# A PEER expert layer: the second token block takes its second-table rows one by one, and all first-table tiles run before the second table

## The chip, the cores and the metric

The kernel runs on one core of a Trainium2 chip. The metric is the device time in microseconds, from the first to the last instruction; three runs gave 1636.88 to 1640.48 us, the median is 1637.82 us.

## What is computed

One decoder layer on 512 tokens of 1024 numbers, in float32: a token-mixing part (attention in a window beside causal pooling), then a retrieval part (PEER) over 128 x 128 = 16384 experts, then a norm. The change is in the retrieval part alone. It picks 16 experts for each of 8 heads and each token, 128 in all, and for each takes a dot product with the expert's row of a first table `u`, and adds the expert's row of a second table `v` with that weight:

```python
def chunk(xc):                                   # 128 tokens
    q = (xc @ w_query).reshape(c, PEER_HEADS, 2, D_HALF)
    sc = jnp.einsum('chpd,hpkd->chpk', q, sub_keys)
    sv, si = lax.top_k(sc, PEER_TOPK)            # 16 of 128 keys, in both halves
    ...                                          # 256 sums, the 16 best
    idx = jnp.take_along_axis(cidx, fi, axis=-1) # expert = 128 i + j
    g = jax.nn.softmax(fv, axis=-1)
    u = u_tab[idx]
    a = jax.nn.gelu(jnp.einsum('chkd,cd->chk', u, xc), approximate=False)
    vv = v_tab[idx]
    return jnp.einsum('chk,chkd->cd', (g * a), vv)
```

## The kernel before

The 512 tokens are four blocks of 128. Block 0 (`GB`) is done by fetching: `gather` fetches for each of its 128 slots one row of 4 KB per token from `u` with an indirect DMA that POOL issues (128 rows, 512 KB), takes the dot product on VectorE (L715), and later fetches the row of `v` and adds it, weighted, to `hg` (L719). Four buffers hold rows (`ROWS`).

Blocks 1 to 3 (`ND` = 3, 384 columns) are done densely. A **first-table tile** (`u_part`) multiplies 128 experts' rows of `u` with all 384 tokens on TensorE, and ScalarE applies Gelu (L604). A **second-table tile** (`v_mm`) multiplies 128 experts' weights, [expert, token], with 128 rows of `v`, and adds into three accumulators in PSUM. There are 128 tiles of either kind. Each product is three matmuls of a high and a low part (`mm3`), so a first-table tile has 8 x 3 = 24 matmuls of 384 columns and a second-table tile 3 x 2 x 3 = 18 of 512. The parts are made by ScalarE, which casts (L118), and VectorE, which subtracts (L110); `w` and `v` tiles have three or two buffers.

What an expert weighs for a token is spread into a dense table by one-hots: `select` finds a block's experts on VectorE, `onehot` builds for eight tokens at a time a one-hot of j (`ohj`) and one of i, weighted (`ohi`), and TensorE multiplies them (`pg`, L584); ScalarE copies the product (`gs`, L585) and SP sends it to DRAM (`spill`). `mix` reads it back (`gt`), multiplies it with the Gelu (L640) and casts (L642). Of every two builds one makes `ohj` on ScalarE (eight Abs of 128 columns, one Relu of 1024), the other on VectorE (`OHN`, `OHA`).

The order: a scheduler places the instructions of the routing stage on in-order queues; in the second-table stage TensorE, VectorE and ScalarE keep the order of the code (`manual_schedule`). `Background` gives out the steps of the selections, of the one-hots and of the fetches in credits for each first-table tile: 2.9 of routing (`R_A`) and 1.1 fetches (`G_A`). So 104 first-table tiles run before and while the routing runs, then comes the second table, and the last 24 first-table tiles stand inside it (`G_V`, `G_B` set the fetches there). Results of the first table that are made ahead lie in SBUF (14 tiles, `RES`) or go to DRAM and back (`ahead`).

## Time and profile before

| | |
|---|---|
| median of three runs | 1637.82 us |
| span of the profiled execution | 1638.0 us |
| TensorE busy | 1593.2 us, 97% |
| VectorE busy | 1260.9 us, 77% |
| ScalarE busy | 760.3 us, 46% |
| POOL busy | 323.0 us, 20% |
| moved by DMA | 403.43 MB, mean 246 GB/s |

A busy share is a mean over stages; for TensorE it is the time in which any matmul's record runs, and records overlap, so the pace is read from how many matmuls a stretch holds. The stages: mixing to about 350 us, scores to 475, block 0's selection to 530, the selections and one-hots of the dense blocks with first-table tiles to 986, the second table to 1620, the last norms.

### The profile page before, as it was taken

The numbers are of one execution on the slowest core, as the hardware profiler recorded it, in microseconds if no ns is written. First come the engines' busy times: TensorE is split into PE (matmuls) and PEld (weight loads), VectorE is DVE, ScalarE is ACT, GpSimd is POOL, SyncE is SP. The second block draws the span as 40 slices with busy tenths as digits, with TensorE's granted clock in tenths as the row PEclk, the third lists the DMA queues.
The fourth block names the chain that finished last, engine by engine and source line by source line (L and its number), as shares of the span: only waits on it lengthen the run. The fifth ranks groups of instructions, "written<-read, shape, count | busy, mean of one in ns | idle before, by whom it ended". The sixth has DMA issues, their size and how long they took to land.

```text
span 1638.0 us, 23397 instructions
## 1 busy us (share of the span) xinstructions
PE 1593.2 (97%) x8389; PEld 1411.9 (86%) x8389; DVE 1260.9 (77%) x2614; ACT 760.3 (46%) x1197; POOL 323.0 (20%) x262
## 2 busy tenths in 40 slices
PE   7999999999999899999999999999999999999997
PEld 6777788888899899999999998878888888899996
DVE  4676433546799899999999866877878878888885
ACT  4655533333333333894598863333333333433334
POOL 0000000000000334223322221221222222244440
PEclk9999999999999999999999999999999999999999
DMA  6111222531324888888988889999999999999983
GB/s 218 65 65 52 78 92 101 180 116 65 116 91 140 296 305 295 300 310 307 312 313 308 289 299 345 300 340 352 349 337 346 359 336 342 338 327 335 323 293 115
DMA packets 168117, 403.43 MB, mean 246 GB/s; under 512 B 14784, under 2 KB 87232, under 8 KB 164800
## 3 DMA queue, kind: packets, MB, share of 16 engines
q1 hardware_dynamic: 130384, 265.07, 46.1%
q0 software_dynamic: 36864, 134.23, 23.9%
q10 hardware_dynamic: 752, 2.62, 0.5%
q8 instruction: 66, 1.08, 0.3%
q14 instruction: 51, 0.42, 0.1%
HBM read 354.81 MB, written 46.53 MB: 245 GB/s over the span
## 4 chain that ended last, share of the span: by engine, by line
PE 86%; DMA 4%; DVE 4%; ACT 4%; issue 2%; SPq 0%; POOL 0%; DVEq 0%; ACTq 0%; POOLq 0%
PE mm L105 16%; PE mm L106 15%; PE mm L107 15%; PE acc L106 10%; PE acc L107 10%; PE acc L105 9%; PE pg L584 5%; DMA vr<-v_experts 2%; PE ho L105 1%; PE ho L107 1%; PE ho L106 1%; PE pss L453 1%; PE mm L368 1%; DVE wl L110 1%; ACT ohj L568 1%
## 5 line engine op out<-in xcount | busy, mean ns | idle before, releaser
L105 PE MATMUL mm<-xh,wh 128*128 128x384 f32 (+2 forms) x1424 | 503.3, 354 | 11.5 <-ACT ga L604 9.3
L107 PE MATMUL mm<-xh,wl 128*128 128x384 f32 (+2 forms) x1424 | 495.1, 348 | 1.9 <-DVE wl L110 1.9
L106 PE MATMUL mm<-xl,wh 128*128 128x384 f32 (+2 forms) x1424 | 494.8, 348 | 0.6 <-DVE xl L110 0.6
L110 DVE TENSOR_TENSOR wl<-wr,wh 128x1024 fp32r<-128x1024 f32 x187 | 228.0, 1220 | 135.7 <-ACT wh L118 123.0
L118 ACT CAST wh<-wr 128x1024 fp32r<-128x1024 f32 x187 | 195.6, 1047 | 284.9 <-PE mm L106 249.4
L709 POOL DMA_INDIRECT row<-u_experts,ei x128 | 150.0, 1172 | 885.5 <-ACT wh L118 528.2
L106 PE MATMUL acc<-vl,wh 128*128 128x512 f32 x768 | 299.9, 391 | 2.4 <-DVE vl L110 2.2
L107 PE MATMUL acc<-vh,wl 128*128 128x512 f32 x768 | 299.4, 390 | 0.0
L105 PE MATMUL acc<-vh,wh 128*128 128x512 f32 x768 | 298.8, 389 | 0.0
L105 PEld LDWEIGHTS mm<-xh,wh 128*128 128x128 f32 x1424 | 270.1, 190 | 31.0 <-ACT ga L604 10.7
L107 PEld LDWEIGHTS mm<-xh,wl 128*128 128x128 f32 x1424 | 269.8, 189 | 16.4 <-DVE wl L110 2.7
L106 PEld LDWEIGHTS mm<-xl,wh 128*128 128x128 f32 x1424 | 270.4, 190 | 13.8 <-DVE xl L110 1.1
L709 POOL DMA_INDIRECT row<-v_experts,ei x128 | 172.3, 1346 | 388.3 <-DVE hg L719 354.8
L642 ACT CAST wh<-wf 128x384 fp32r<-128x384 f32 x128 | 65.8, 514 | 322.5 <-PE acc L106 236.1
L110 DVE TENSOR_TENSOR vl<-vr,vh 128x1024 fp32r<-128x1024 f32 x128 | 156.7, 1224 | 52.8 <-ACT vh L118 49.7
L106 PEld LDWEIGHTS acc<-vl,wh 128*128 128x128 f32 x768 | 144.2, 188 | 33.9 <-DVE vl L110 4.6
L107 PEld LDWEIGHTS acc<-vh,wl 128*128 128x128 f32 x768 | 144.2, 188 | 29.8
L105 PEld LDWEIGHTS acc<-vh,wh 128*128 128x128 f32 x768 | 144.2, 188 | 29.5
L719 DVE SCALAR_TENSOR_TENSOR hg<-row,act,hg 128x1024 f32<-128x1024 f32 x128 | 163.6, 1278 | 2.9 <-DMA row<-v_experts,ei 2.5
L715 DVE SCALAR_TENSOR_TENSOR row<-row,natg 128x1024 f32<-128x1024 f32 x128 | 155.5, 1216 | 8.8 <-DMA row<-u_experts,ei 8.8
L118 ACT CAST vh<-vr 128x1024 fp32r<-128x1024 f32 x128 | 134.1, 1048 | 24.4 <-DMA vr<-v_experts 17.8
L110 DVE TENSOR_TENSOR wl<-wf,wh 128x384 fp32r<-128x384 f32 x128 | 74.0, 578 | 42.1 <-ACT wh L642 40.8
(179 smaller groups left out, 1611.6 us busy)
## 6 DMA issues: line engine op xcount, KB each, us to landing
wr<-u_blocks SPq DMA_DIRECT2D x128, 512.0 KB
vr<-v_experts SPq DMA_DIRECT2D x128, 512.0 KB
spill<-gs SPq DMA_DIRECT2D x24, 1024.0 KB
gt<-spill SPq DMA_DIRECT2D x64, 384.0 KB
ahead<-ga SPq DMA_DIRECT2D x90, 192.0 KB
gar<-ahead SPq DMA_DIRECT2D x90, 192.0 KB
wr<-w_in SPq DMA_DIRECT2D x30, 512.0 KB
wr<-w_query SPq DMA_DIRECT2D x16, 512.0 KB
```

Source lines behind the costliest of these rows:

```text
L105: mm(out, lhsT=l[0], rhs=r[0], start=first, stop=False)
L106: mm(out, lhsT=l[0], rhs=r[1], start=False, stop=False)
L107: mm(out, lhsT=l[1], rhs=r[0], start=False, stop=last)
L110: self.lowered = self.nc.vector.tensor_tensor(lo, src, hi.bitcast(F32), op=ALU.subtract).ins
L118: self.nc.scalar.copy(hi, raw)
L368: nc.tensor.matmul(po[half * 64:half * 64 + 64], lhsT=vn[:, b - 1 + k, kv * 64:kv * 64 + 64], rhs=pT[:, k, 2 * half:2 * half + 2, :], star ...
L453: nc.tensor.matmul(pss[n][b // 2][:, b % 2, i - n, :], lhsT=qT[:, b * P:(b + 1) * P], rhs=subk[:, i, :], start=True, stop=True)
L584: nc.tensor.matmul(pg[:, z, :], lhsT=ohj[:, z, :], rhs=ohi[:, z, :], start=True, stop=True)
L642: nc.scalar.copy(wh, wf)
L709: nc.gpsimd.indirect_dma_start(out=t, out_offset=None, in_=tab, in_offset=bass.IndirectOffsetOnAxis(ap=ei[:, s:s + 1], axis=0))
L715: nc.vector.scalar_tensor_tensor(u, u, 1.0, xn2, op0=ALU.mult, op1=ALU.mult, accum_out=act[:, s:s + 1])
L719: nc.vector.scalar_tensor_tensor(z, v, act[:, s:s + 1], z, op0=ALU.mult, op1=ALU.add)
```

## The change

Block 1 (`LB`) is taken out of the second table. Its first table stays dense: a tile still has 384 columns (`TU`), but the Gelu of block 1's 128 columns is written to a DRAM array of its own, `late`, [expert, token], four tiles at a time (`AJ`). Once all of it is there, `gather_late` fetches each of block 1's 128 x 128 activations singly: an indirect DMA for each slot takes one element per token, at the address 128 expert + token (`ea`). VectorE scales them and adds the fetched rows of `v` to `h1`. The dense second table, its one-hots and gates cover blocks 2 and 3 (`NV` = 2, 256 columns).

All 128 first-table tiles run before the second table. Block 0's fetches are given 2.3 credits a tile and are ended with the first table. 90 tiles' results stay in SBUF (4, 40 and 46), 38 go through DRAM. `ohj` is made by ScalarE in every build, now with the gate's weight in it (a second activation for each of the eight tokens), and `ohi` on VectorE by one comparison over 1024 columns in place of eight.

```diff
-ND = 3
+LB = 1
+VB = 2
+NV = 2
+TU = SEQ - P
+TD = NV * P
+AJ = 4
-R_A = 2.9
-G_A = 1.1
+R_A = 3.0
+G_A = 2.3
+LAG = 8
+R_F = 2.9
+KEEP = 4
+HELD = (40, 46)
-OHN, OHA = 2, 1
...
         def build(n):
-            if n % OHN < OHA:
-                for z in range(8):
-                    nc.scalar.activation(ohj[:, z, :], self.iota, AF.Abs, bias=tr[:, 1, u + z:u + z + 1])
-                nc.scalar.activation(ohj, ohj, AF.Relu, bias=1.0, scale=-1.0)
-            else:
-                v.tensor_tensor(ohj, iob, tr[:, 3, u:u + 8].unsqueeze(2).to_broadcast([P, 8, P]), op=ALU.is_equal)
+            for z in range(8):
+                nc.scalar.activation(ohj[:, z, :], self.iota, AF.Abs, bias=tr[:, 1, u + z:u + z + 1])
+            for z in range(8):
+                nc.scalar.activation(ohj[:, z, :], ohj[:, z, :], AF.Relu, bias=tr[:, 2, u + z:u + z + 1],
+                                     scale=tr[:, 3, u + z:u + z + 1])
-            for z in range(8):
-                v.tensor_scalar(ohi[:, z, :], self.iota, tr[:, 0, u + z:u + z + 1], tr[:, 2, u + z:u + z + 1],
-                                op0=ALU.is_equal, op1=ALU.mult)
+            v.tensor_tensor(ohi, iob, tr[:, 0, u:u + 8].unsqueeze(2).to_broadcast([P, 8, P]), op=ALU.is_equal)
...
+    def u_part(self, n, w, xn2):
+        ps = self.project(w, xn2, slice(LB * P, LB * P + TU))
+        if n % AJ == 0:
+            self.a1 = self.ga.tile([P, AJ, P], F32, name="a1", bufs=2)
+        nc.scalar.activation(self.a1[:, n % AJ, :], ps[:, :P], AF.Gelu)
+        if n % AJ == AJ - 1:
+            nc.sync.dma_start(out=self.late.rearrange("(n j t) o -> n j (t o)", j=P, t=P)[n - AJ + 1:n + 1]
+                              .rearrange("n j t -> j n t"), in_=self.a1)
...
+        nc.scalar.activation(ga, ps[:, P:], AF.Gelu)
...
+    def dense(self, acc, fetch):
+        rate = PH * TOPK / (NKEY - 3 - LAG)
         for n in range(NKEY):
             m = n + 1
+            if m < NKEY:
+                step = self.mix(m)
                 next(step)
                 next(step)
                 v_low = self.v_load(m)
+                if m >= LAG:
+                    fetch.spend(rate)
                 next(step, None)
                 v_low()
             self.v_mm(n, self.ws.pop(n), self.vs.pop(n), acc)
...
+    def gather_late(self, ei, ea, g, z):
+        act = self.dp.tile([P, PH * TOPK], F32, name="act1", bufs=1)
+        def elem(s):
+            nc.gpsimd.indirect_dma_start(out=act[:, s:s + 1], out_offset=None, in_=self.late,
+                                         in_offset=bass.IndirectOffsetOnAxis(ap=ea[:, s:s + 1], axis=0))
+        for k in range(TOPK):
+            elem(k)
+        yield 0
+        for h in range(PH):
+            hs = slice(h * TOPK, (h + 1) * TOPK)
+            nc.vector.tensor_tensor(act[:, hs], act[:, hs], g[:, hs], op=ALU.mult)
+            for s in range(h * TOPK, (h + 1) * TOPK):
+                if h + 1 < PH:
+                    elem(s + TOPK)
+                v = self.rows_of(self.a["v_experts"], ei, s)
+                nc.vector.scalar_tensor_tensor(z, v, act[:, s:s + 1], z, op0=ALU.mult, op1=ALU.add)
+                yield 1
...
-            bg = Background(choose(1), choose(2), spread(1), choose(3), spread(2), spread(3))
+            bg = Background(choose(2), choose(3), spread(2), choose(LB), spread(3))
...
+        rest = (2 * PH * TOPK - fetch.spent) / max(1, NKEY - ahead)
+        while ahead < NKEY:
+            with tc.issue_after(part()):
+                fetch.spend(rest)
+        fetch.spend(1e9)
```

The engines' queues show what the scheduler makes of it at three places. On ScalarE, in a one-hot stage, the kernel before has this (`wh` are casts of first-table weights, `ga` Gelus, `gs` copies of a product):

```order
L585 COPY gs_5915<-pg_5916 128x8x128
L568 ACTIVATE ohj_5963<-iota_155,tr3_5753 128x128 x8
L569 ACTIVATE ohj_5963<-ohj_5963 128x1024
L118 CAST wh_6145<-wr_6144 128x1024
L604 ACTIVATE ga_5960<-mm_5935 128x384
L585 COPY gs_5915<-pg_5982 128x8x128
L585 COPY gs_6004<-pg_6005 128x8x128
L568 ACTIVATE ohj_6052<-iota_155,tr3_5753 128x128 x8
L569 ACTIVATE ohj_6052<-ohj_6052 128x1024
L118 CAST wh_6234<-wr_6233 128x1024
L604 ACTIVATE ga_6049<-mm_6024 128x384
```

The changed kernel, in the second half of its first one-hot stage (`a1` is the Gelu of block 1):

```order
L603 ACTIVATE a1_6450<-mm_6425 128x128
L612 ACTIVATE ga_6452<-mm_6425 128x256
L570 ACTIVATE ohj_6455<-iota_155,tr3_5866 128x128 x8
L572 ACTIVATE ohj_6455<-ohj_6455,tr3_5866 128x128 x8
L585 COPY gs_6399<-pg_6474 128x8x128
L121 CAST wh_6845<-wr_6844 128x1024
L738 ACTIVATE act_4535<-act_4535 128x16
L603 ACTIVATE a1_6450<-mm_6499 128x128
L612 ACTIVATE ga_6525<-mm_6499 128x256
L570 ACTIVATE ohj_6528<-iota_155,tr3_5866 128x128 x8
L572 ACTIVATE ohj_6528<-ohj_6528,tr3_5866 128x128 x8
L585 COPY gs_6547<-pg_6548 128x8x128
```

Between two copies stand sixteen activations of 128 columns in place of none, or eight and one long one. In the first half of this stage eight builds follow each other with two casts among them and no Gelu.

On POOL, where the second table begins, the kernel before goes on with block 0's rows:

```order
L709 DMA row_9244<-v_experts,ei0_2733 128x1024
L709 DMA row_9281<-u_experts,ei0_2733 128x1024
L709 DMA row_9302<-v_experts,ei0_2733 128x1024
L709 DMA row_9336<-u_experts,ei0_2733 128x1024
L709 DMA row_9370<-v_experts,ei0_2733 128x1024
L709 DMA row_9404<-u_experts,ei0_2733 128x1024
```

The changed kernel has block 1's single elements there, 128 of them among the first 36 rows of `v`:

```order
L690 DMA row_10400<-v_experts,ei0_2733 128x1024
L690 DMA row_10445<-v_experts,ei1_2734 128x1024
L690 DMA row_10651<-v_experts,ei1_2734 128x1024
L690 DMA row_10681<-v_experts,ei1_2734 128x1024
L699 DMA act1_10426<-late,ea_2741 128x1 x20
L690 DMA row_10710<-v_experts,ei1_2734 128x1024
L699 DMA act1_10426<-late,ea_2741 128x1
L690 DMA row_10739<-v_experts,ei1_2734 128x1024
L699 DMA act1_10426<-late,ea_2741 128x1 x31
L690 DMA row_10768<-v_experts,ei1_2734 128x1024
```

A row whose turn comes after a group of single elements is issued after them.

On VectorE, at the same place, the kernel before has this (`wf` is a gate product, `vl` a split of the second table):

```order
L110 TENSOR_TENSOR wl_9249<-wr_9247,wh_9248 128x1024
L715 SCALAR_TENSOR_TENSOR row_9281,act_4502<-row_9281,natg_2379 128x1024
L640 TENSOR_TENSOR wf_9057<-gk0_2970,gt_9052 128x384
L640 TENSOR_TENSOR wf_9292<-gk1_3241,gt_9052 128x384
L719 SCALAR_TENSOR_TENSOR hg_76<-row_9302,act_4502,hg_76 128x1024
L110 TENSOR_TENSOR wl_9059<-wf_9057,wh_9058 128x384
L110 TENSOR_TENSOR wl_9294<-wf_9292,wh_9293 128x384
L110 TENSOR_TENSOR vl_9299<-vr_9297,vh_9298 128x1024
L640 TENSOR_TENSOR wf_9326<-gk2_3512,gt_9052 128x384
L715 SCALAR_TENSOR_TENSOR row_9336,act_4502<-row_9336,natg_2379 128x1024
```

In the changed kernel, where the second table's splits are named `wl<-wr`, it is this:

```order
L751 TENSOR_TENSOR ssf_10453<-ssf_10453 128x1
L753 RECIPROCAL rf_10455<-sdf_10454 128x1
L755 SCALAR_TENSOR_TENSOR fin_10452<-hg_76,rf_10455,gfin_10409 128x512 x2
L647 TENSOR_TENSOR wf_10423<-gk0_2978,gt_10418 128x256
L647 TENSOR_TENSOR wf_10469<-gk1_3250,gt_10418 128x256
L115 TENSOR_TENSOR wl_10425<-wf_10423,wh_10424 128x256
L115 TENSOR_TENSOR wl_10471<-wf_10469,wh_10470 128x256
L115 TENSOR_TENSOR wl_10476<-wr_10474,wh_10475 128x1024
L647 TENSOR_TENSOR wf_10494<-gk2_3522,gt_10418 128x256
L707 TENSOR_TENSOR act1_10426<-act1_10426,gw1_2738 128x16
L712 SCALAR_TENSOR_TENSOR h1_10411<-row_10445,act1_10426,h1_10411 128x1024
L115 TENSOR_TENSOR wl_10496<-wf_10494,wh_10495 128x256
```

The seventh row from the first `wf` on scales the first 16 single activations of block 1 and stands ahead of the splits for the third tile; the addition of a row, in each tile of the kernel before, is there in one tile of the first seven.

## Rows read from the trace of the kernel before

**Rows 1.** The page: engine, busy us (share of the span), x instructions.

```profile
PE 1593.2 (97%) x8389; PEld 1411.9 (86%) x8389; DVE 1260.9 (77%) x2614; ACT 760.3 (46%) x1197; POOL 323.0 (20%) x262
```

**Rows 2.** Busy time by stretch: us, engines (x instructions), granted clock, DMA share, GB/s.

```profile
core 0: us, PE busy (x) PEld busy (x) DVE busy (x) ACT busy (x) POOL busy (x), PEclk, DMA share, GB/s
...
530.00:661.00 131.00, 123.45 (x694) 121.74 (x693) 122.87 (x314) 47.45 (x65) 56.81 (x37) 0.97 0.88 298
...
798.00:986.00 188.00, 182.87 (x1233) 181.36 (x1232) 159.42 (x357) 155.53 (x238) 47.33 (x34) 1.00 0.85 302
993.00:1420.00 427.00, 423.63 (x1861) 350.08 (x1862) 345.84 (x457) 152.74 (x211) 93.81 (x97) 1.00 0.98 340
1420.00:1620.00 200.00, 200.00 (x1012) 182.09 (x1011) 161.04 (x190) 76.28 (x106) 80.78 (x60) 1.00 0.85 299
1620.00:1638.00 18.00, 7.68 (x34) 6.00 (x32) 9.70 (x20) 6.47 (x18) 0.00 (x0) 0.77 0.25 94
```

**Rows 3.** Groups by shape: busy us, mean ns | idle us before, and its releaser.

```profile
L118 ACT CAST wh<-wr 128x1024 fp32r<-128x1024 f32 x187 | 195.6, 1047 | 284.9 <-PE mm L106 249.4 <-issue 24.2 <-DVE wl L110 5.4
...
L585 ACT COPY gs<-pg 128x1024 f32<-128x1024 f32 x48 | 94.2, 1993 | 11.8 <-PE pg L584 11.8
...
L584 PE MATMUL pg<-ohi,ohj 128*128 128x128 f32 x768 | 92.2, 276 | 4.5 <-ACT ohj L569 4.5
...
L568 ACT ACTIVATE ohj<-iota,tr 128x128 f32<-128x128 f32 x192 | 58.5, 394 | 1.4 <-DVE tr L558 1.3
...
L604 ACT ACTIVATE ga<-mm 128x384 f32<-128x384 f32 x114 | 55.3, 485 | 60.5 <-PE mm L107 60.5
...
L569 ACT ACTIVATE ohj<-ohj 128x1024 f32<-128x1024 f32 x24 | 25.4, 1057 | 0.6
```

**Rows 4.** VectorE's timeline, second table: start, us, instruction [idle before].

```profile
1214.65 0.55 DVE L640 TENSOR_TENSOR wf<-gar,gt 128x384 f32<-128x384 f32 x1
1215.12 1.27 DVE L719 SCALAR_TENSOR_TENSOR hg<-row,act,hg 128x1024 f32<-128x1024 f32 x1
1216.32 0.55 DVE L110 TENSOR_TENSOR wl<-wf,wh 128x384 fp32r<-128x384 f32 x1
1216.81 1.23 DVE L110 TENSOR_TENSOR vl<-vr,vh 128x1024 fp32r<-128x1024 f32 x1
1217.95 0.55 DVE L640 TENSOR_TENSOR wf<-gar,gt 128x384 f32<-128x384 f32 x1
```

**Rows 5.** ScalarE's timeline, in a one-hot stage and beside rows 4.

```profile
911.67 1.05 ACT L118 CAST wh<-wr 128x1024 fp32r<-128x1024 f32 x1 [1.45 <-PE mm L106]
...
1215.31 0.52 ACT L642 CAST wh<-wf 128x384 fp32r<-128x384 f32 x1 [3.53 <-DVE wf L640]
1215.73 1.05 ACT L118 CAST vh<-vr 128x1024 fp32r<-128x1024 f32 x1
```

**Rows 6.** Timeline of POOL, and of VectorE, where rows are fetched.

```profile
1430.54 0.94 POOL L709 DMA_INDIRECT row<-u_experts,ei  x1 [0.30 <-issue]
1431.79 1.30 POOL L709 DMA_INDIRECT row<-v_experts,ei  x1 [0.30 <-issue]
...
1437.64 1.23 DVE L715 SCALAR_TENSOR_TENSOR row<-row,natg 128x1024 f32<-128x1024 f32 x1 [0.22 <-DMA row<-u_experts,ei]
```

**Rows 7.** Busy time of two shorter stretches, columns as in rows 2.

```profile
1170.00:1180.00 10.00, 10.00 (x46) 8.29 (x45) 8.36 (x12) 3.43 (x5) 2.37 (x3) 1.00 1.03 402
1200.00:1250.00 50.00, 49.50 (x219) 40.66 (x218) 40.15 (x55) 17.80 (x25) 10.54 (x11) 1.00 1.00 351
```

**Rows 8.** The page, DMA queues: packets, MB, share of 16 engines.

```profile
q1 hardware_dynamic: 130384, 265.07, 46.1%
```

**Rows 9.** VectorE's timeline at the start of the second table.

```profile
992.44 1.03 DVE L640 TENSOR_TENSOR wf<-gk,gt 128x384 f32<-128x384 f32 x2 [4.32 <-DMA gt<-spill]
```

More of the change, by code (lines that the diff above doesn't have):

```diff
@@ L89, in consts @@
         self.iota = self.const("iota", a["iota"].partition_broadcast(P), [P, P])
+        self.tok = self.c.tile([P, 1], I32, name="tok")
+        self.nc.sync.dma_start(out=self.tok, in_=a["tok"])
     def pool(self, name, bufs, **kw):
@@ L624, in v_mm @@
     def v_mm(self, n, w, v, acc):
-        for c in range(ND):
+        for c in range(NV):
             sl = slice(c * P, (c + 1) * P)
@@ L664, in open_dense @@
         return finish
-    def dense(self, ahead, xn2, acc, fetch):
-        us = {}
-        def u_load(m):
-            if ahead <= m < NKEY:
-                us[m] = self.weights(self.a["u_blocks"][m])
-        def rate(m):
-            return G_V if m < ahead else G_B
-        last = NKEY - 2
-        scale = (2 * PH * TOPK - fetch.spent) / sum(rate(m) for m in range(1, last))
-        for m in (0, 1):
-            u_load(m)
+    def dense(self, acc, fetch):
+        rate = PH * TOPK / (NKEY - 3 - LAG)
         for n in range(NKEY):
             m = n + 1
-            if m == NKEY:
-                pass
-            elif m < ahead:
-                step = self.mix(m, ahead)
+            if m < NKEY:
+                step = self.mix(m)
                 next(step)
@@ L793, in part @@
                     after = self.lowered
-                self.u_part(ahead, w, xn2, True)
+                self.u_part(ahead, w, xn2)
                 ahead += 1
                 return after
-            for i, _ in enumerate(self.scores(xn2, tp, sv, si, subk)):
-                if i % U_S == U_S - 1:
-                    part()
+            with tc.tile_pool(name="score", bufs=1, side="right", reuse_waits="tile") as sp:
+                subk = sp.tile([P, 16, P], F32, name="subk")
+                nc.scalar.dma_start(out=subk, in_=a["sub_keys"])
+                for i, _ in enumerate(self.scores(xn2, sp, sv, si, subk)):
+                    if i % U_S == U_S - 1:
+                        part()
+            self.home, self.room = self.pool("held", 1, reuse_waits="tile"), HELD[0]
             first = Background(self.select(tp, sv[GB], si[GB], ei[GB], gw[GB]))
-            bg = Background(choose(1), choose(2), spread(1), choose(3), spread(2), spread(3))
+            bg = Background(choose(2), choose(3), spread(2), choose(LB), spread(3))
             fetch = Background(self.gather(GB, nat[GB], ei[GB], gw[GB]))
-            while not bg.done or ahead < AHEAD:
+            while not bg.done:
                 after = part()
@@ L807, in run @@
                     if not first.done:
-                        first.spend(R_A)
+                        first.spend(R_F)
                     else:
@@ L811, in run @@
                         fetch.spend(G_A)
+        self.home, self.room = self.pool("more", 1, reuse_waits="tile"), HELD[1]
+        rest = (2 * PH * TOPK - fetch.spent) / max(1, NKEY - ahead)
[3 more added lines that the diff above has]
+        fetch.spend(1e9)
+        self.xs.close()
         with tc.tile_pool(name="dense", bufs=2, reuse_waits="tile") as self.dp:
             dp = self.dp
-            acc = [self.big([P, 2, 512], "acc") for _ in range(ND)]
-            mix = self.open_dense()
+            acc = [self.big([P, 2, 512], "acc") for _ in range(NV)]
             gf = dp.tile([P, D], F32, name="gfin", bufs=1)
             nc.sync.dma_start(out=gf, in_=a["ln_final_g"].partition_broadcast(P))
-            for _ in range(TAIL):
-                with tc.issue_after(part()):
-                    fetch.spend(G_A)
+            h1 = dp.tile([P, D], F32, name="h1", bufs=1)
+            nc.sync.dma_start(out=h1, in_=self.hspill[0])
+            mix = self.open_dense()
+            late = Background(self.gather_late(ei[LB], ea, gw[LB], h1))
+            late.spend(0.01)
             mix()
+            self.final(GB, self.hg, gf)
             with tc.manual_schedule(engines={mybir.EngineType.PE, mybir.EngineType.DVE, mybir.EngineType.Activation}):
-                self.dense(ahead, xn2, acc, fetch)
-            fetch.spend(1e9)
-            self.final(GB, self.hg, gf)
-            for c in range(ND):
-                hb = dp.tile([P, D], F32, name="hb", tag="vr", bufs=RAW)
-                nc.sync.dma_start(out=hb, in_=self.hspill[c])
-                self.final(DB + c, hb, gf, acc[c])
+                self.dense(acc, late)
+            late.spend(1e9)
+            self.final(LB, h1, gf)
+            for c in range(NV):
+                hb = self.w.tile([P, D], F32, name="hb", tag="wr", bufs=RAW)
+                nc.sync.dma_start(out=hb, in_=self.hspill[VB - LB + c])
+                self.final(VB + c, hb, gf, acc[c])
 class Background:
```

101 lines of the change are left out of this document (44 added, 57 removed).

## The prediction

> **What bounds the kernel now.** I read the page's busy shares first, then the stretches by stage, then the groups by shape, and last the timelines of single tiles. TensorE is busy 97% of the span, but that does not say that every stage has slack elsewhere [rows 1]. By stage [rows 2]: the stretch 993 to 1420 us is the second-table product on three token blocks, with 1861 matmuls, so 1861/18 = 103.4 tiles in 427 us, 4.13 us a tile and 1.38 us for a tile and block. In 1420 to 1620 us a tile has 24 first-table matmuls besides the 18: 1012/42 = 24.1 tiles, 8.30 us each, which leaves 8.30 - 4.13 = 4.17 us for a first-table tile. TensorE is the bound in both. It isn't far from others, though: VectorE is busy 346 of 427 us there and 123 of 131 us while the selections run (530 to 661), ScalarE 156 of 188 us while one-hots are built (798 to 986), and the DMA rings carry 340 GB/s with a share of 0.98 [rows 2].
>
> **What TensorE is relieved of.** Block 1 leaves the second table: 128 x 1.38 = 177 us. Its one-hot products go too, a third of 92.2 us of records; a build's eight products take 1.9 us, so 16 builds are 30 us [rows 3]. With TensorE alone as the bound the kernel would take 1638 - 207 = 1431 us. What comes in its place goes to other engines: 128 more row fetches from the second table (64 MB in all, 128 VectorE additions), 128 fetches of single elements on POOL, ScalarE's whole one-hot of j, and all first-table tiles stand ahead of the second table, so that the two stages no longer share their loads. So I go stage by stage, and take the largest engine of each. The span is 1638.0 us and the median of the three runs 1637.82, so no correction is needed.
>
> **Up to 530 us** nothing changes but one piece: the order of VectorE now puts block 0's last score work and half its selection ahead of one weight split, some 20 us in a row, where TensorE holds three tiles of 4.17 us in hand. I charge 5 us (bounds 0 and 10): 535 us.
>
> **Selections of blocks 2 and 3.** Before, this stretch is 131 us with VectorE busy 122.9 [rows 2]. The changed order has the same pieces and 46 rows where 36 stood (G_A 2.3 for 1.1): 10 x 1.2 us more (the addition of a row, to the next start) [rows 4], 135 us. Then come four tiles in whose VectorE rows 17 row fetches, eight compares and products and four sums stand: 17 x 1.2 + 12 x 0.95 + 4 x 1.2 = 36 us against 4 x 4.17 = 17 us of TensorE, since the scheduler put them ahead of the one-hot. Sum 171, to 706 us.
>
> **The two one-hot stages are ScalarE's now.** One activation of 128x128 takes 58.5/192 = 0.305 us; a copy of the product 1.99 us [rows 3]. A build had eight of the first, one over 1024 columns (1.06 us) and the copy, and only every second one was ScalarE's. Now each has sixteen and the copy: 16 x 0.305 + 1.99 = 6.87 us, sixteen builds 110 us. A tile adds a cast (1.05) and two smaller activations in place of one of 0.485 (at most twice that, I take 0.7) [rows 3, 5]. The order has 11 tiles in the first stage: 110 + 11 x 1.75 = 129 us. In its second half every cast also waits for a tile whose last matmuls stand among the one-hot products, as the cast at 911.67 waits 1.45 us [rows 5]; short activations overlap a little at their ends. I take 130 (bounds 126 and 139). TensorE has 11 x 4.17 + 30 = 76 us in it and stands idle for the rest. The second such stage has 13 tiles: 142 (131 to 149). Block 1's selection between them has 11 tiles, 46 us at TensorE's pace. This brings us to 706 + 130 + 46 + 142 = 1024 us.
>
> **The rest of the first table.** 42 tiles, with 102 row fetches. Four buffers hold rows, and a fetch that starts at 1430.54 is used at 1437.64, when VectorE has just waited for it: 7.1 us, and 1.2 us until the buffer is free [rows 6]. Four rows in 8.3 us, 2.43 rows a tile: 5.0 us a tile. TensorE's floor is 4.17. Bytes: 0.52 + 2.43 x 0.52 + 0.06 = 1.86 MB a tile, 5.3 us at the 351 GB/s of the busiest 50 us, 4.6 us at the 402 GB/s of the busiest 10 us [rows 7]. I take 4.75: 200 us, to 1224 (bounds 175 and 223).
>
> **The opening of the second table** has a new wait. VectorE's seventh row of the stage scales the first 16 single activations, and all that follows on VectorE waits behind it, the weights of tile 2 first. The fetches can't start before the last four tiles' activations are in DRAM, which is queued on SP behind four loads: some 8 us (before, the same place waits 4.32 us for gates) [rows 9]. Then POOL issues 20 of them: POOL starts one every 1.25 us when it waits for nothing (1430.54, 1431.79: 0.94 busy and 0.30 of issue) [rows 6]. This price is of a fetch of 128 rows of 4 KB; no row shows one of 128 single elements. From below it may be 0.94; I take 1.25 because the list of addresses is as long. So 8 + 16 x 1.25 + some 6 for landing (the 7.1 us less an issue) = 34 us in which TensorE has two tiles. And POOL's order goes on against the stage: 128 single fetches and 32 rows stand up to row 35, so 8 + 160 x 1.25 + 6 = 214 us, where VectorE would be at that row's tile, the 39th, after 34 + 37 x 3.15 = 151 us. Tile 39 is thus done 214 us after the first table's end, at 1438.
>
> **The other 89 tiles.** Per tile TensorE has 2 x 1.38 = 2.75 us. VectorE's cycle for three blocks is seen where it catches up: from 1214.65 to 1217.95, 3.30 us for gate product, row addition, two splits [rows 4]; ScalarE's two casts lie inside it, and the next gate product waits for them through the split [rows 4, 5]. With 256 columns for 384 the two small ones lose a third of some 0.4 us each (0.27), and 1.09 rows for 1 add 0.11: 3.15. The bytes are 0.52 for the table, 0.57 for rows, 0.13 for gates and 0.04 reloaded = 1.27 MB; at 351 GB/s 3.61 us, at 402 GB/s 3.15. I take 3.3, as the bursts show that 351 is no ceiling: 294 us, to 1732. From the last matmul to the end 12 us (1620 to 1638 holds it [rows 2]): 1744. Single elements cost the rings between nothing and the time of a mean packet (46.1% of 16 rings' 1638 us over 130384 packets is 93 ns; eight on each ring for a fetch, 0.74 us) [rows 8]; they lie in the stretch that POOL bounds, so I charge none.
>
> The Trainium skill ("DMA: Bandwidth & Descriptors", Specifications) gives about 358 GB/s as what HBM yields a core, and says under Where 436 GB/s comes from that this side binds for HBM to SBUF. The trace has no 50 us over 351, but 10 us at 402 [rows 7]; by the page's rule the kernel would take the time of the second rival.
>
> **Rivals.** *Faster:* the engines' work lies under one another and each stage runs at the sum of its largest engine: 530 + 135 + 25 + 126 + 46 + 126 + 175 = 1163 us to the end of the first table; single fetches at 0.94 us that no one waits for beyond the opening (20 us), 126 tiles at 3.15 = 397, and 12: 1592. For it: VectorE and ScalarE do run back to back in places [rows 4, 5]. Against it: the queues are in order, and the one-hot stages hold 126 us by ScalarE alone. It decides from a POOL start of about 1.0 us and a stage tile under 3.2. *The rings are the ceiling at 351 GB/s:* 42 x 0.55 + 89 x 0.31 = 51 us more, 1795. For it: a share of 1.00 in that stretch; against it 402 GB/s in a shorter one [rows 7]. *TensorE's clock:* idle between one-hot products it may fall to the lower level, 1.2 of 2.4 GHz; the granted clock was 1.00 in the stretches with steady work, 0.97 in the selections and 0.77 at the end, where TensorE is idle for more than half [rows 2]. Tiles of 8.3 us would then make a build and tile 8.3 + 3.8 = 12.1 us against ScalarE's 6.87 + 1.75 + 1.2 = 9.8: 24 x 2.3 = 55 us, 1799. *The relief doesn't reach the end time and nothing is lost:* 1634.5 to 1641, by chance alone.
>
> **How the numbers follow.** A measurement of this kernel tells about 0.2% from no change, 3.3 us. My forecast (1660 to 1775) has 0.52; the ceiling of the rings or the clock, or both in part (1775 to 1830) 0.23; above that 0.05; the faster rival 0.17; no change 0.03. So faster 0.17, same 0.03, slower 0.80. The range leaves out the upper 0.05 and most of the faster case: 1620 to 1830.
>
> **What would show it.** Right: in the two one-hot stages ScalarE busy over 90% and TensorE near 60%; the first table ends near 1224 us; VectorE waits some 20 us behind the first scaling, for single fetches; POOL is busy in the first 200 us of the second table and VectorE waits for rows; later tiles every 3.3 us with VectorE busiest and the rings at 370 to 390 GB/s. Wrong: if single fetches start every microsecond or less, the 39th tile comes 60 us earlier; if they take longer, later; if TensorE stays over 90% busy from 530 us on, the whole reasoning falls.

## The result, and the profile after

The changed kernel takes 1848.6 us (median of four runs, 1844.74 to 1853.51) against 1638.31 us: a ratio of 1.1287, 95% interval 1.1263 to 1.1310. It is slower, as forecast, but by 210 us and not by 106; the time lies 18.6 us above the range. The profiled run has a span of 1843.0 us.

The page of the kernel after, busy time by engine; it answers to [rows 1]. TensorE is busy 66 us less, and POOL 299 us more:

```profile
PE 1527.4 (83%) x7362; PEld 1303.2 (71%) x7362; DVE 1285.6 (70%) x2368; ACT 814.6 (44%) x1605; POOL 621.5 (34%) x518
```

Its busy time by stage, as in [rows 2] (us, each engine's busy time with its instructions, granted clock, DMA share, GB/s). The cuts are the stages of the prediction:

```profile
core 0: us, PE busy (x) PEld busy (x) DVE busy (x) ACT busy (x) POOL busy (x), PEclk, DMA share, GB/s
425.00:547.00 122.00, 110.60 (x579) 103.44 (x578) 106.30 (x507) 41.04 (x72) 4.29 (x4) 0.94 0.37 112
547.00:718.00 171.00, 153.78 (x826) 150.15 (x825) 163.13 (x357) 60.04 (x121) 87.04 (x64) 0.96 0.91 315
718.00:855.00 137.00, 89.51 (x488) 85.83 (x487) 88.89 (x179) 128.27 (x295) 52.44 (x39) 0.79 0.76 265
855.00:905.00 50.00, 47.57 (x269) 47.01 (x268) 48.44 (x62) 18.25 (x40) 25.48 (x19) 1.00 0.99 344
905.00:1054.00 149.00, 107.70 (x601) 102.71 (x600) 76.45 (x85) 134.27 (x314) 49.17 (x36) 0.85 0.72 248
1054.00:1281.00 227.00, 193.29 (x998) 186.27 (x996) 171.67 (x189) 64.08 (x130) 130.75 (x99) 0.94 0.94 339
1281.00:1522.00 241.00, 137.15 (x469) 100.54 (x469) 119.32 (x160) 54.50 (x84) 181.18 (x165) 0.80 0.64 203
1522.00:1830.00 308.00, 272.59 (x1050) 195.96 (x1051) 277.91 (x365) 124.14 (x182) 90.45 (x89) 0.97 0.98 349
1830.00:1843.00 13.00, 4.38 (x18) 2.92 (x16) 7.09 (x13) 3.43 (x11) 0.00 (x0) 0.81 0.30 116
```

Read it by the largest busy time of each row. From 547 us on the stages have different owners: VectorE in the selections (163 of 171 us), ScalarE in the one-hots (128 of 137, 134 of 149). From 1054 to 1281 us no engine is near full (TensorE 193 of 227). From 1281 to 1522 POOL is the busiest (181 of 241, and 54 us more of issue before its instructions) while TensorE and VectorE stand idle for almost half of it, and at the end VectorE is (278 of 308). Before, TensorE was the busiest in each of the stretches up to 1620 us, in the selections only just [rows 2].

| stage | forecast, us | measured, us | difference |
|---|---|---|---|
| up to the selections of blocks 2 and 3 | 535 | 547 | +12 |
| selections of blocks 2 and 3 | 171 | 171 | 0 |
| one-hot of block 2 | 130 | 137 | +7 |
| selection of block 1 | 46 | 50 | +4 |
| one-hot of block 3 | 142 | 149 | +7 |
| rest of the first table | 200 | 227 | +27 |
| opening, to tile 39 of the second | 214 | 241 | +27 |
| other tiles of the second table | 294 | 308 | +14 |
| tail | 12 | 13 | +1 |

The stages went in the order that was told, and nearly each took longer than told. The experiments ask whether each is held by what the prediction named.

### The profile page after: what moved, and what is told of

The parts are those of the page before. It is cut to its first block, busy times and chain, and to the rows that moved or that the text cites. A ratio compares the mean times of both kernels' runs of the same rounds, so it can differ in the third digit from the quotient of the medians.

```text
span 1843.0 us, 21921 instructions
## 1 busy us (share of the span) xinstructions
PE 1527.4 (83%) x7362; PEld 1303.2 (71%) x7362; DVE 1285.6 (70%) x2368; ACT 814.6 (44%) x1605; POOL 621.5 (34%) x518
## 5 line engine op out<-in xcount | busy, mean ns | idle before, releaser
L121 ACT CAST wh<-wr 128x1024 fp32r<-128x1024 f32 x315 | 330.1, 1048 | 467.9 <-PE mm L111 332.4
L115 DVE TENSOR_TENSOR wl<-wr,wh 128x1024 fp32r<-128x1024 f32 x315 | 384.8, 1222 | 200.6 <-ACT wh L121 191.4
L690 POOL DMA_INDIRECT row<-v_experts,ei x256 | 316.1, 1235 | 404.1 <-DVE h L712 183.3
L111 PE MATMUL acc<-wl,wh 128*128 128x512 f32 x512 | 225.3, 440 | 115.3 <-DVE wl L115 112.8
L110 PE MATMUL acc<-wh 128*128 128x512 f32 x512 | 211.7, 413 | 28.4 <-ACT wh L649 16.1
L111 PEld LDWEIGHTS acc<-wl,wh 128*128 128x128 f32 x512 | 102.7, 201 | 181.7 <-DVE wl L115 162.6
L712 DVE SCALAR_TENSOR_TENSOR h<-row,act,h 128x1024 f32<-128x1024 f32 x128 | 163.9, 1280 | 92.5 <-DMA row<-v_experts,ei 92.1
L112 PE MATMUL acc<-wh,wl 128*128 128x512 f32 x512 | 211.0, 412 | 0.0
L584 PE MATMUL pg<-ohi,ohj 128*128 128x128 f32 x512 | 103.5, 326 | 61.1 <-DVE ohi L575 24.2
L699 POOL DMA_INDIRECT act<-late,ea x128 | 137.3, 1073 | 46.6 <-issue 44.1
```

The costliest lines, as they stand in the source:

```text
L110: mm(out, lhsT=l[0], rhs=r[0], start=first, stop=False)
L111: mm(out, lhsT=l[0], rhs=r[1], start=False, stop=False)
L112: mm(out, lhsT=l[1], rhs=r[0], start=False, stop=last)
L115: self.lowered = self.nc.vector.tensor_tensor(lo, src, hi.bitcast(F32), op=ALU.subtract).ins
L121: self.nc.scalar.copy(hi, raw)
L584: nc.tensor.matmul(pg[:, z, :], lhsT=ohj[:, z, :], rhs=ohi[:, z, :], start=True, stop=True)
```

## Experiments

The edits are shown shortened; `...` and plain words stand for code left out.

### The one-hots as before

```
+  if n % 2 < 1:
       for z in range(8):
           nc.scalar.activation(ohj[:, z, :], self.iota, AF.Abs, bias=tr[:, 1, u + z:u + z + 1])
-      for z in range(8):
-          nc.scalar.activation(ohj[:, z, :], ohj[:, z, :], AF.Relu, bias=tr[:, 2, ...], scale=tr[:, 3, ...])
+      nc.scalar.activation(ohj, ohj, AF.Relu, bias=1.0, scale=-1.0)
+  else:
+      v.tensor_tensor(ohj, iob, tr[:, 3, ...], op=ALU.is_equal)
-  v.tensor_tensor(ohi, iob, tr[:, 0, ...], op=ALU.is_equal)
+  for z in range(8):
+      v.tensor_scalar(ohi[:, z, :], self.iota, tr[:, 0, ...], tr[:, 2, ...], op0=ALU.is_equal, op1=ALU.mult)
```

> The changed kernel with the one-hots built as before the change: every second j table is a VectorE comparison, the others take one long Relu on ScalarE, and the weight g goes onto the i table by eight 128x128 VectorE operations. Everything else is as changed. Theory (the two one-hot stages, 137 and 149 us long, are ScalarE's): ScalarE loses 8 x (8 x 0.305 - 1.06) + 8 x 16 x 0.305 = 50 us of its 128 in the first stage and is no bound any more; VectorE gains 128 x 0.268 - 16 x 1.22 + 8 x 1.22 = 25 us and has 89 + 25 = 114 there, 76 + 25 = 101 in the second, where TensorE has 108. So the stages fall to some 116 and 110 us: 60 us less in all, about 1788 us. Rival (the stages are long because TensorE's granted clock is 0.79 and 0.85 in them, whoever feeds it, or because of the order of the instructions): less than 20 us, 1830 us or more.

Measured: 1803.82 us, 45 us less. Busy time by stage in this run, from block 2's one-hot on (columns as above):

```profile
718.00:812.00 94.00, 87.43 (x571) 85.65 (x572) 89.49 (x198) 74.86 (x129) 37.61 (x26) 0.98 0.92 340
812.00:893.00 81.00, 59.33 (x282) 56.79 (x281) 73.22 (x165) 21.24 (x40) 46.51 (x31) 0.83 0.89 298
893.00:989.00 96.00, 76.56 (x456) 73.07 (x454) 88.20 (x192) 66.83 (x114) 38.27 (x28) 0.86 0.88 309
989.00:1228.00 239.00, 197.52 (x1010) 188.52 (x1010) 175.22 (x195) 63.77 (x129) 143.03 (x106) 0.94 0.94 333
```

The two one-hot stages fall from 137 and 149 to 94 and 96 us, so ScalarE did hold them; VectorE (89 of 94, 88 of 96) holds them now. The rival of the clock falls too, though the granted clock was indeed lower in these stages (0.79 and 0.85): the second is 53 us shorter at a granted clock of 0.86, against 0.85. But the selection between them takes 81 us in place of 50: in the changed kernel about half of block 1's selection ran on VectorE beside block 2's one-hot and 16 us of it between the one-hots, and here nearly all of it, 32 us, stands between them. And the rest, up to the last tile but one, takes 239 us; in the changed kernel that is 1054 to 1271, 217 us. Of 96 us won, 45 reach the end. What makes the rest longer shows when it is counted from the last copy of a one-hot product on: here the matmuls of 42 tiles and 106 row fetches in 240 us, in the changed kernel those of 43 tiles and 101 fetches in 230. That is 2.26 and 2.27 us a fetch, so the pace goes by the row and not by the tile.

### Single fetches left out, and single fetches in time

Left out:

```
-  for each of 128 columns: indirect DMA of 128 single elements into act[:, s]
+  one plain DMA of 128 x 128 elements into act
```

> The changed kernel with the 128 fetches of single activations left out: one plain DMA of 128x128 elements of the same DRAM table fills the tile, so the factors of block 1's rows are wrong numbers; the rows are fetched and added as before. Theory (POOL's 160 starts at 1.25 to 1.5 us set the first 39 second-table tiles, which took 229 us): tile 39 comes at the pace of the later ones, 8 us for the opening and 39 x 3.3 to 3.6 = 129 to 140 us, so 80 to 95 us less in all, 1750 to 1768 us; POOL busy under 100 us in the stage and no wait of VectorE for a row longer than 6 us in a steady pattern. Rival (the row fetches themselves, with four buffers, or the DMA rings set these tiles, not the single fetches): less than 25 us, over 1820 us.

Kept, in the order of the code:

```
-  manual_schedule(engines={PE, DVE, Activation})
+  manual_schedule(engines={PE, DVE, Activation, Pool})
   for k in range(16): elem(k)
-  yield 0        # the first scaling follows at once, at tile 2
+  yield 1        # it follows at tile 8, with the first row
```

> The changed kernel with GpSimd's instructions of the second-table stage kept in the order in which the code is written (as TensorE's, VectorE's and ScalarE's are), and the first 16 activations scaled at tile 8, where the first row is due, not at tile 2. So POOL issues one single fetch and one row fetch in turn, 1.09 of each a tile: 2 x 1.09 x 1.25 = 2.7 us of POOL a tile. Theory (the 160 starts that the scheduler put ahead of the rows are the bound of the first 39 tiles, and the work itself is not): almost all of what leaving them out gives, 60 to 90 us less, 1755 to 1785 us; all second-table tiles at 3.3 to 3.6 us. Rival (a single fetch costs the same wherever it stands, or delays the row behind it, so that POOL's 2.7 us plus waits for a row buffer set the pace): 4.3 us a tile and more over 119 tiles, no gain, 1830 to 1870 us.

Measured: 1761.84 us without them (one run), and 1759.57 us with all of them in order (1.0742 of before, 1.0711 to 1.0772). So leaving the work out gains no more than putting it in time. The second run makes two changes at once; what the later scaling is worth by itself was not tried. The same two stretches, opening to tile 39 and from there to the last split, first without the fetches, then with them in order:

```profile
1289.00:1438.00 149.00, 122.81 (x475) 88.51 (x473) 119.88 (x163) 59.08 (x90) 39.80 (x38) 0.93 0.94 324
1438.00:1748.00 310.00, 273.64 (x1054) 195.62 (x1055) 278.21 (x366) 124.63 (x182) 95.61 (x90) 0.98 0.98 353
```

```profile
1280.00:1429.00 149.00, 124.51 (x475) 90.14 (x473) 119.22 (x163) 59.03 (x90) 110.19 (x91) 0.92 0.92 318
1429.00:1738.00 309.00, 272.56 (x1051) 193.96 (x1052) 279.46 (x367) 124.89 (x182) 197.12 (x166) 0.98 1.00 357
```

Both win 92 us in the first stretch and nothing in the second. In the run with the fetches POOL is busy 197 us of the second stretch in place of 96 and it takes 309 us in place of 310: a single fetch has no price for VectorE's pace or the rings that these runs can see. Its whole price in the changed kernel is its place in POOL's queue. That place in the changed kernel, first the waits of 1281 to 1522 us (who <- for whom: us in all, times, longest):

```profile
ACT wh L649 <- DVE wf L647: 153.2, 32, 25.6
PEld acc L111 <- DVE wl L115: 97.1, 32, 24.4
DVE h L712 <- DMA row<-v_experts,ei: 91.9, 30, 23.9
PE acc L111 <- DVE wl L115: 82.8, 23, 24.0
POOL act L699 <- issue: 44.1, 120, 7.9
```

then VectorE's timeline at the opening (start, us, instruction, idle before it and its releaser):

```profile
1295.09 0.42 DVE L647 TENSOR_TENSOR wf<-gk,gt 128x256 f32<-128x256 f32 x1
1308.80 0.18 DVE L707 TENSOR_TENSOR act<-act,gw 128x16 f32<-128x16 f32 x1 [13.30 <-DMA act<-late,ea]
1309.01 1.28 DVE L712 SCALAR_TENSOR_TENSOR h<-row,act,h 128x1024 f32<-128x1024 f32 x1
```

VectorE waits 92 us for rows that POOL started late, and ScalarE, TensorE and the next products stand behind it; at the opening it waits 13.3 us at the scaling for the sixteenth single fetch.

### Half rows

```
-  t <- 128 rows of 4 KB
+  t[:, :512] <- 128 half rows of 2 KB, read twice by the same VectorE operation
-  HELD = (40, 46)
+  HELD = (36, 46)
```

> The changed kernel with every row fetch, of both tables and both blocks, cut to 128 rows of 2 KB in place of 4 KB (a half row of the same list, so the results of blocks 0 and 1 are wrong numbers); the number of fetches and VectorE's operations on 1024 columns stay, each half being read twice. Theory A (the DMA rings, at 340 to 350 GB/s, are the ceiling of the 42 remaining first-table tiles, 5.4 us each, and of the last 89 tiles, 3.55 us each): the bytes fall from 1.86 to 1.22 and from 1.27 to 0.99 MB a tile, so TensorE's 4.2 to 4.4 us and VectorE's 3.07 us take over: 42 x 1.0 + 89 x 0.45 = 82 us less, about 1765 us. Theory B (a fetch's latency with four row buffers sets the first of the two, VectorE's own queue the second): under 25 us less, over 1820 us. Between them: one stage each, and the stage's own time tells which.

Measured: 1775.94 us (one run), 73 us less. Its stretches 40 tiles before the end of the first table, opening to tile 39, and 70 of the last tiles:

```profile
1039.00:1224.00 185.00, 178.43 (x983) 175.62 (x982) 162.49 (x181) 61.06 (x126) 133.15 (x96) 0.98 0.81 263
1228.00:1480.00 252.00, 146.45 (x478) 106.35 (x476) 120.14 (x163) 58.36 (x90) 176.06 (x166) 0.76 0.51 153
1524.00:1748.00 224.00, 211.77 (x842) 152.36 (x841) 222.70 (x292) 95.72 (x141) 78.74 (x74) 1.00 0.92 305
```

The same tiles took 5.40 us in the changed kernel and take 4.63 here; the last ones 3.53 and now 3.20, with VectorE busy 222.7 of 224 us. The stretch that POOL holds is no shorter at 153 GB/s (252 us against 241): bytes don't matter there. For the first table the run can't tell bytes from latency, since a half row also landed sooner (4.6 to 5.1 us in the median from its issue, against 6.9 to 7.2).

### Six row buffers

```
-  ROWS = 4;  HELD = (40, 46)
+  ROWS = 6;  HELD = (33, 46)
```

> The changed kernel with six buffers for fetched rows in place of four; to make room, 33 tiles of activations of the second hold stay in SBUF in place of 40 (seven more go out to DRAM and come back, 0.9 MB each way). It separates the two theories of the 42 first-table tiles after the one-hots that half rows left mixed (they fell from 5.41 to 4.63 us, and a half row may also land sooner). Theory A (the rings' rate is the bound): no change there, 5.2 to 5.4 us a tile, the last 89 tiles at 3.5 to 3.6, in all 1838 to 1855 us. Theory B (four buffers and a fetch's 8.3 us are the bound): 6 rows in 8.3 us are 3.4 us a tile, so TensorE's 4.2 to 4.4 us decides, 40 us less, about 1805 us.

Measured: 1815.6 us (one run), 33 us less. 40 tiles of the rest of the first table, first in the changed kernel, then with six buffers:

```profile
1055.00:1271.00 216.00, 187.75 (x969) 181.38 (x968) 165.27 (x181) 60.18 (x123) 127.94 (x97) 0.94 0.95 342
```

```profile
1034.00:1216.00 182.00, 175.47 (x979) 173.63 (x978) 160.81 (x178) 60.31 (x124) 129.49 (x95) 0.99 1.03 407
```

4.55 us a tile, TensorE busy 96%, and 407 GB/s. So neither 342 GB/s nor a DMA share of 0.95 was a ceiling there. Theory A falls for this stage, and B stands: four buffers for rows, each in use from a fetch's start until VectorE is done with the row. 97 fetches started in 216 us, one every 2.23 us, so a buffer's round was 8.9 us. Read fetch by fetch, the trace gives the same: in the median 8.6 us from a fetch's start to the end of VectorE's operation on the row, and 0.28 us more to the start of the next fetch into that buffer. The waits agree; in the changed kernel in this stretch (four of its rows):

```profile
POOL row L690 <- DVE hg L726: 41.5, 37, 2.8
DVE hg L726 <- DMA row<-v_experts,ei: 30.4, 29, 3.1
POOL row L690 <- DVE row L722: 25.8, 20, 4.2
DVE row L722 <- DMA row<-u_experts,ei: 19.1, 19, 2.4
```

POOL waits for VectorE to free a buffer and VectorE waits for the row that POOL couldn't start: each for the other, with no engine full. The last tiles of the second table gain nothing from six buffers (3.59 us).

### Five load buffers

```
   raw tiles of the second table's loads:      3 -> 5 buffers
   activations reloaded from DRAM:             3 -> 5 buffers;  HELD = (38, 36)
```

> The changed kernel with five buffers for the loads of the second table and for reloaded activations in place of three (for the room, twelve tiles of activations fewer are kept in SBUF, 1.5 MB more each way). It asks why the last 89 tiles take 3.5 us and not VectorE's 3.07 to 3.18 us: half rows gave 3.20, six row buffers nothing (3.59). Theory A (the rings are full at 350 to 360 GB/s in this stage): no change but the 1.5 MB, 3.5 to 3.6 us a tile, 1845 to 1858 us. Theory C (a load lands 6.1 us after its issue, is cast and split in 2 to 3 us more, and with three buffers that makes one load in 3 us or more; as with the row buffers in the first table, it is latency over buffers): 3.2 us a tile, some 30 us less, 1815 to 1825 us.

Measured: 1836.35 us (one run), 12 us less. Seventy of the last tiles take 3.36 us each, between the two theories; in the runs with three buffers they take 3.51 to 3.63. The changed kernel, then this run; the DMA rows are: what, engine's queue, times, KB each, median us from issue to landing:

```profile
1571.00:1818.00 247.00, 218.21 (x843) 156.41 (x842) 223.55 (x292) 96.86 (x141) 76.75 (x74) 0.98 0.99 356
wr<-v_experts SPq DMA_DIRECT2D x70, 512.0 KB, 6.1
```

```profile
1574.00:1809.00 235.00, 214.65 (x836) 155.48 (x837) 222.70 (x290) 95.58 (x141) 76.52 (x73) 0.98 1.04 382
wr<-v_experts SPq DMA_DIRECT2D x70, 512.0 KB, 9.2
```

More loads in flight (with more reloaded activations; the two weren't separated) raise the rate by 7%, from 356 to 382 GB/s, and each then lands half as late again. So in this run half of what lies between 3.53 us and VectorE's 3.18 was latency over three buffers; for the other half the longer landing speaks for full rings, at some 380 GB/s with this mix of transfers, but no run fixed that number, and the last run below does not repeat the gain.

### The reordering alone

```
 (kernel before)
-  AHEAD = 60
+  AHEAD = 122
```

> The kernel before with one number changed: all first-table tiles run ahead of the second table (AHEAD 122 and 6 more, for 60 and 6). Three blocks stay dense, so it is the reordering part of the change alone; 62 more tiles of activations (three blocks, 0.197 MB each) go out to DRAM and come back. Theory (the reordering costs little by itself as long as TensorE has three blocks of products per tile: 4.13 us a tile against VectorE's 3.3 us, and bytes of 0.52 for the table, 0.57 for 1.1 rows, 0.2 for gates and 0.2 reloaded, 1.49 MB a tile, which is 361 GB/s at 4.13 us, just above the 340 to 350 seen over long stretches): 1640 to 1690 us. Rival (the reordering itself takes from TensorE its reserve of work, so that the losses of the changed kernel, in the first table and in the second, come with it): above 1720 us.

Measured: 1642.0 us, 1.0014 of before (1.0002 to 1.0026). Its busy line:

```profile
PE 1596.7 (97%) x8389; PEld 1413.3 (86%) x8389; DVE 1257.6 (77%) x2614; ACT 757.0 (46%) x1195; POOL 313.3 (19%) x262
```

All first-table tiles ahead of the second table cost 0.14% with three dense blocks. (104 ran ahead before, so 24 tiles are moved, as in the changed kernel, and not the 62 of the expectation.) So the order of the tables alone loses nothing; the loss comes with the rest of the change. That TensorE's smaller work per tile no longer covers the others fits the stage table, but no run tried it alone.

### Putting the parts together

> The two edits together: one-hots built as before the change (45 us less alone) and GpSimd's instructions in the order of the code (89 us less alone). Theory (they act in different stages, whose losses add up): 1848 - 45 - 89 = 1714 us, 1705 to 1725. Rival (they share a bound, say the rings, which would be reached in both): 1730 us or more.

Measured: 1722.85 us (1.0477, 1.0409 to 1.0546), 126 us less. The two gains, 45 and 89 us, add up but for 8 us; the four runs lie 25 us apart.

```
-  bg = Background(choose(2), choose(3), spread(2), choose(1), spread(3))
+  bg  = Background(choose(2), choose(3), choose(1))      # 2.2 a tile
+  hot = Background(spread(2), spread(3))                 # 1.3 a tile, from jf[2] on
   (GpSimd in order, as above)
```

> GpSimd's instructions in the order of the code, as in the run before, and the changed kernel's own one-hots (all of j on ScalarE), but they no longer stand in stages of their own: they run beside the selections of the next blocks, over 76 first-table tiles in place of 67 (block 2's one-hot beside the selections of block 3 and 1, block 3's behind it). No work is added but nine more tiles that go out to DRAM and back. Theory (each stage of the changed kernel is held by one engine while the others idle: VectorE in the selections, ScalarE in the one-hots; summed over the stretch VectorE has 376 + 9 x 4.1 = 413 us, ScalarE 354, TensorE 377): the stretch that took 556 us takes 420 to 450 and the kernel 1640 to 1670 us, about the time of before. Rival (the queues are in order and the one-hots share their four buffers with the selections, so they wait for one another): less than 50 us gained on 1760 us, above 1710.

Measured: 1703.22 us (1.0382, 1.0365 to 1.0399): 56 us less than in order alone, half of what was expected. The stretch with one-hots took 488 us with TensorE busy 415 and VectorE 411, 85 and 84%. Were row buffers part of the miss? The same with six of them:

> The run with one-hots beside selections and GpSimd in the order of the code, with six row buffers in place of four (33 tiles kept in place of 40). In that run the first-table tiles after the opening took 5.2 to 5.9 us each, with VectorE, ScalarE and TensorE all under 90% busy. Theory (four row buffers over a fetch's latency, 2.2 us a row and 2.35 rows a tile, held these tiles too): 4.6 us a tile as six buffers gave in the changed kernel, 0.6 to 0.8 us times 109 tiles = 65 to 85 us less, 1620 to 1640 us, beside or just under the kernel before. Rival (there the queues of VectorE and ScalarE wait for one another through the shared buffers of one-hots and selections): only the 28 tiles after the one-hots gain, 25 us, 1675 to 1685 us.

Measured: 1633.45 us (0.9975, 0.9948 to 1.0003), as the theory had it and level with the kernel before. The first table now ends at 1158 us in place of 1219. Last, six buffers for the second table's loads:

> The run beside it with six buffers for second-table loads and five for reloaded activations (31 + 31 tiles kept). By theory C of the five-buffer run 0.3 us of each of 119 tiles goes, 30 to 35 us less than the run beside it: 1585 to 1610 us, faster than both kernels; by theory A nothing, or a few us more.

Measured: 1629.25 us, 0.9945 of before (0.9928 to 0.9963): faster than both kernels, by half a per cent over the kernel before, but the step over the run beside it is only 4 us, less than that run's own spread (1630.23 to 1641.74). Its stages:

```profile
547.00:1005.00 458.00, 405.45 (x2342) 396.00 (x2341) 409.08 (x721) 349.21 (x787) 249.84 (x177) 0.95 0.96 354
1005.00:1152.00 147.00, 143.02 (x782) 141.49 (x781) 130.17 (x143) 49.91 (x99) 104.81 (x74) 0.97 1.03 404
1307.00:1614.00 307.00, 272.07 (x1055) 197.05 (x1054) 280.40 (x369) 123.45 (x182) 199.67 (x165) 0.97 0.99 359
```

In the first row TensorE, VectorE and ScalarE are busy 89, 89 and 76%; in the changed kernel, from 547 to 1054 us, it is 79, 74 and 67%. The last row is the changed kernel's 308 us still: here six load buffers did not lift the rate (359 GB/s), and a load landed 11.3 us after its issue in the median. Why five did lift it in the run above and six don't here stays open; single fetches run in this stretch here and did not there.

## Why the forecast was right in kind and short in size

**The direction was right, and so were the stages' owners.** ScalarE in the one-hots and POOL in the opening stood the test; VectorE in the selections reads that way, but no run tried it. The selection term of 171 us came out to the microsecond, and some of that is luck: the cut at 547 us is where 17 first-table tiles are done, as at 530 before, but block 2's selection starts at 543.4. The faster rival needed the engines' work to lie under one another; it does so only where the order of the code is changed for it.

**One-hots, +7 each: the price of one activation, and casts that wait.** The prediction took 0.305 us for all sixteen activations of a build, from the Abs of [rows 3]. The groups after, by shape (busy us, mean ns of one | idle before), show that the Abs kept its price (78.3/256 = 0.306 us of busy time), and that the short Relu, which reads its scale and bias from the table and works in place, takes 102.1/256 = 0.399 us:

```profile
L572 ACT ACTIVATE ohj<-ohj,tr 128x128 f32<-128x128 f32 x256 | 102.1, 489 | 0.0
L570 ACT ACTIVATE ohj<-iota,tr 128x128 f32<-128x128 f32 x256 | 78.3, 397 | 3.0 <-DVE tr L561 2.9
```

That is 128 x 0.094 = 12 us a stage more than priced. An operation with other operands was given the nearest row's price without a margin. But other operations of the stages cost less (the records of neighbours overlap), and ScalarE's busy time, 128 and 134 us, is nearly what the prediction's terms give, 129 and 110 + 13 x 1.75 = 133. What is over is ScalarE's idle time, 9 and 15 us, most of it casts that wait for TensorE's matmuls, in the first stage and then in the second:

```profile
ACT wh L121 <- PE mm L111: 6.0, 5, 3.9
ACT wh L121 <- PE mm L111: 14.1, 7, 4.7
```

The prediction named this wait and, less the overlaps, took 1 us for it in the first stage. The 142 us that it took for the second is 9 over its own terms, and it says not for what.

**Rest of the first table, +27: the choice of 4.75 us.** Three numbers were in hand: TensorE's 4.17, the row buffers' 5.0, and the rings' 4.6 to 5.3. When several things bound a stage, its time is at least the largest, and 4.75 lay under the buffers' 5.0. That number itself was short: it came from one fetch with a round of 8.3 us; measured it was 8.9, 5.4 us a tile. This is the step that failed first: the bound was in the prediction, and the sum went under it. The rival of the rings at 351 GB/s had 5.3 us for these tiles and so was nearly right in number, but wrong in cause: six buffers carried 407 GB/s. Nor was 351 GB/s the most of 50 us before: that holds for slices cut at full fifties, and from 1356 to 1406 us the kernel before carried 368. The rule from the Trainium skill that the prediction set beside it ("DMA: Bandwidth & Descriptors", Specifications: about 358 GB/s from HBM for a core) is passed by the row with 407. The Trainium skill says elsewhere ("Perfetto Trace Analysis", Roofline) that this figure is a core's share when both cores of a pair access the memory, and that one core alone may reach some 120% of it. 407 GB/s is 114% of 358, so the row agrees with that.

**Opening to tile 39, +27: POOL's start.** The price of 1.25 us was right for a POOL that has the machine to itself: from 1286.95 us on most fetches start every 1.25 us. But once VectorE works again, they start slower: 160 starts took 224 us, 1.40 us each and not 1.25, and tile 39's split came 11 us after the last of them. The bounds named for this price went below it (0.94) and not above. The opening itself was shorter than told: the scaling came 28 us after the first table's end and not 34, as the sixteenth fetch landed some 2 us after its start and not 6. The place and the mechanism were right, and both experiments gave back 92 us there.

**Last tiles, +14: 3.3 us was between VectorE and the rings.** Measured 3.5. VectorE alone gives 3.18 (half rows), a little over the 3.15 of the sum; the rest is loads that land late. The five-buffer run puts that down to latency over three buffers and to the rings in about equal parts, the last run doesn't, so the split stays open. Again the value was taken between two bounds and not at the larger (3.61 at 351 GB/s).

**Up to 547 us, +12: the largest overrun of a bound (0 to 10).** The waits of 425 to 547 us show TensorE twice without a free product, some 6 us each, behind a Gelu on ScalarE. ScalarE stands behind VectorE, the first time with a copy of scores (`sc`), the second with the selection's softmax (`gw`):

```profile
ACT sc L462 <- DVE si L491: 20.8, 6, 4.6
PEld mm L110 <- ACT gk L612: 12.0, 2, 6.3
ACT gw L528 <- DVE gw L520: 8.6, 1, 8.6
```

So the charge had the cause, VectorE's long piece of work, but not the way to TensorE: TensorE has no wait for a weight split in this stretch, and the three tiles said to be in hand didn't help. Block 0's selection itself ended at 536 us (529 before), but the next one stands behind a later tile's split and started at 543 (before, at once). No run took this apart.

**The errors all have one sign.** Seven of the nine terms were 4 to 27 us short and none was long: 99 us in all on the span, while the upper end of the range allowed 86 (the median lies another 6 us above the profiled span). Every term took its stage as the work of its fullest engine, or a value between two bounds, and what in-order queues lose by waiting for one another came on top. More than half, 54 us, lies in two terms whose mechanism was right and whose size was not: the rows' buffers at 4.75 us a tile in place of 5.4, and POOL's start at 1.25 us in place of 1.40, with the 11 us behind it.

## To carry to other kernels

When a change takes work from the engine that was full, look stage by stage at what that engine's time was hiding: the row buffers and the order on a DMA queue became bounds here though neither was changed on purpose, and so did the short operations that the change moved to another engine. Price a stage at the largest of its bounds plus something, and a ring of buffers at (time from a fetch's start until its last reader is done) / buffers, before calling a steady DMA rate a ceiling. Work that is not in the hand-written order can be put ahead of everything else on its queue: 128 small fetches cost 92 us in front of the rows and nothing between them.

## What the runs showed of the hardware

A core's DMA rings carried 407 GB/s over 182 us with six row buffers, and 404 over 147 us in the last run, against at most 368 in any 50 us of the kernel before (351 in [rows 7]); a DMA share of 0.95 at 342 GB/s did not mean that they were full.

A fetch of 128 single elements costs POOL as much as one of 128 rows of 4 KB (0.94 us undisturbed), and both depend on what VectorE does. POOL's timeline (start, us of one), first in the changed kernel while VectorE waits, then with the fetches in order while VectorE works:

```profile
1297.54 0.94 POOL L699 DMA_INDIRECT act<-late,ea  x1 [0.30 <-issue]
1298.79 0.94 POOL L699 DMA_INDIRECT act<-late,ea  x1 [0.30 <-issue]
```

```profile
1400.24 1.23 POOL L699 DMA_INDIRECT act<-late,ea  x1 [0.30 <-issue]
1401.77 1.22 POOL L690 DMA_INDIRECT row<-v_experts,ei  x1 [0.30 <-issue]
```

Of the changed kernel's 128 single fetches, 55 ran with no VectorE instruction beside them and took 0.94 us each. Slower are those that start while a VectorE instruction runs: these 56 took 1.24 us in the mean, up to 1.90. The 17 during which VectorE began only after the fetch's start took 0.94 to 0.95, though a row addition, with two inputs from SBUF, then ran beside each of them. So such an operation beside a fetch is not enough to slow it. The run with the fetches in order shows the same: 1.25 us (108 fetches) against 0.94 (the other 20). The cause was not tried.
